# Latent attention with the rope query's two parts in one operand, a reordered beginning, FFN edges filled by needed transposes and a full-row bias matmul

## The chip, the cores and the metric

The kernel runs on one core of one Trainium2 chip. The metric is the device time of one execution in microseconds. A core has a matrix engine (TensorE, "PE" in the profile; its weight loads are the row "PEld"), a vector engine (VectorE, "DVE"), a scalar engine (ScalarE, "ACT"), GpSimd ("POOL") and SyncE ("SP"), whose queue issues the DMAs here. Each engine works through its own instructions in order; semaphores tie them together.

## What is computed

A decoder trunk of two layers on 256 tokens of width 1024, all in float32:

```
x <- LN(alpha*x + 0.5*SwiGLU_1(x))              # FFN 1, inner width 2816
x <- LN(alpha*x + Mixer(x))                     # layer 0: forgetting attention (FoX); layer 1: latent attention (MLA)
x <- LN(alpha*x + 0.5*SwiGLU_2(x))              # FFN 2
x <- LN(alpha*x + sigmoid(x Wg + bg) * (p Wp))  # per-layer embedding (PLE)
```

The latent attention has 16 heads. A head's score is a sum of two products: a query and a key of 128 columns each (no position), and a rotated query of 64 columns (rope) with a rotated key of 64 columns that all heads share:

```
c_q = rms_norm(x W_dq);  q = c_q W_uq                  # 16 heads x (128 + 64)
q_rope = rope(q[..., 128:]);  k_rope = rope(x W_kr)    # k_rope is shared by all heads
s = (q_nope . k_nope + q_rope . k_rope) / sqrt(192)    # causal softmax, then times V, then W_o
```

The keys without position and V come from a latent c_kv of 256 columns, formed once from the stream that leaves layer 0.

## The kernel before

**Arithmetic.** Each float32 operand is split into a high part (rounded to the matmul's input type, a copy on ACT) and a low part (the difference, a subtraction on DVE). `parts` (line 490) does this for activations. A product is then three matmuls into one PSUM bank: high x high, high x low, low x high (`mm3`, line 475; the instruction itself is line 483). Transposes are matmuls with an identity (line 487). The 256 tokens are two tiles t = 0, 1 of 128.

**Weights.** All weights stream from HBM once, in the order of their first use, which a dry run of the same program records. SP loads groups into three raw buffers; `Stream.split` (line 152) makes the high part on ACT (line 171) and the low part on DVE (line 172), into one of some ten slots. `pump` (line 240), called after each product, splits the next unit when it has arrived and ACT and DVE are, by a cost model in the source, not too far behind; `fill` (line 138) forces a number ahead; `ahead` (line 131) and `later` (line 147) do the two halves of a split at different places; `hold` forbids `pump`. PSUM has eight banks in three rings: `y` (4), `h` (2), `tr` (2).

**FFN** (`ffn`, line 572). The inner width is 11 chunks of 256. Chunks 0 and 1 are computed per token tile by `H`, with the tokens stationary, and transposed by `T` (line 630). Chunks 2 to 10 are computed by `HT` (line 642) with the weight stationary: four quarters u of 24 matmuls with 256 columns, into two banks of ring `h` (even chunks) or `tr` (odd chunks). `W` (line 668) multiplies a chunk with the output weight, 24 matmuls with 512 columns into the four `y` banks. The order is: H of 0 and 1, T(0), then three groups of three chunks (GROUPS, line 52), each followed by the W of the chunks done so far (0 to 4, then 5 to 7); the W of chunks 8 to 10 come last, for tile 0 and then tile 1, with the layer norms. T(1) stands inside chunk 2, behind its first quarter. Ahead of chunks 5 and 8, `HT` issues transposes of the identity that nobody reads: EDGE (line 53) has four each in FFN 1 and one each in FFN 2. In FFN 2 the PLE's input p is loaded at chunk 4, transposed at chunk 5 (`ple_transpose`, line 727) and projected at chunk 8 (`ple_project`, line 737; its copies to SBUF are line 750). In the FFN 1 of layer 1 the latent key side is transposed behind the first group (`kv_transpose`, line 1144).

**PLE** (`ple`, line 752). The gate's bias is added by two matmuls per block, with a row of ones as the stationary operand and the high and then the low part of the bias as one row (lines 756 to 763). Blocks are 512 columns, except four quarters of 256 for tile 1 of the last layer, whose eight bias matmuls stand together.

**Latent attention** (`mla`, line 1167). The beginning forms c_q (`dq`, `cq_transpose`), the rope queries (`q_rope`, `rope`; the sums of line 1237 are on GpSimd or DVE) and transposes them into `xT`, where high and low part are separate operands of 128 rows, two heads to an operand. `V` forms values, `gen(h)` (line 1242) query and key of head h. Then a loop over heads, written out by hand: gen(h+1), T(h-1) (transpose of the softmax's result P, line 1299), QK(h) (line 1260), softmax(h) (line 1276; its last step, line 1294, is on GpSimd), O(h-2) (product with the output weight, 12 matmuls), AV(h-1) (line 1316). QK has, for each of two query tiles (128 and 256 keys), three matmuls of query and key and three of rope query and rope key; the operand of the rope key is zero in the 64 rows of the pair's other head.

## Time and profile before

| | |
|---|---|
| runs shown | 1098.92, 1098.73, 1095.04 us; median 1098.73 |
| the profiled execution | 1100.22 us, its span 1098.2 us |
| mean granted TensorE clock | 0.997 |
| HBM read | 196.81 MB, 180 GB/s over the span |
| 16 DMA engines, share of the span on the weight queue | 55.6% |
| chain of work that ended last | PE 88%, DVE 5%, DMA 2%, ACT 2% |

In a row of a group, the names say output<-inputs, the shapes follow, then the count; behind the bar stand busy time in us, the mean length of one in ns, and the idle time of the engine just ahead of them with what ended it. The length of a matmul is longer than its distance to the next, because matmuls overlap in the array; the distance from start to start is what one costs. A row of the timeline has start, length in us, engine, line, operation, names and count. A row of the waits view has waiting engine, line and operation, the one waited for, us in total, times, and the longest.

### The profile page before, as it was taken

The page shows a single profiled execution, that of the slowest core. Times are in us where ns is not written, and L with a number is a line of the kernel's source. Part 1 is how long each engine was busy: PE and PEld are TensorE (multiplying, and loading weights), DVE is VectorE, ACT ScalarE, POOL GpSimd, SP SyncE. Part 2 cuts the span into 40 slices and gives each one's busy share as a digit, 9 for nine tenths or more (in the row PEclk, how much of TensorE's full clock was granted, in tenths as well). Part 3 has the DMA queues.
Part 4 walks back from the last instruction along what each step waited for, and adds up shares of the span by engine and source line. Part 5 has one row for each costly group of instructions (what it writes and reads, how often), then busy time and mean ns, then how long its engine had stood idle before and what let it go on. Part 6 is the DMA issues. An engine that isn't in the chain of part 4 may idle for free.

```text
span 1098.2 us, 17696 instructions
## 1 busy us (share of the span) xinstructions
PE 1080.7 (98%) x7186; PEld 978.4 (89%) x7186; DVE 713.3 (65%) x1010; ACT 542.2 (49%) x792; POOL 75.6 (7%) x126
## 2 busy tenths in 40 slices
PE   9999999999999999999999999999999999999997
PEld 6989999899879999997899899988999789898986
DVE  5765545788897545448976463487766885554576
ACT  5654443657645444434565353355655474444421
POOL 0000000223200000000220000011111000000000
PEclk9999999999999999999999999999999999999999
DMA  8886652454458766455577654444443578555502
GB/s 276 282 293 224 209 188 82 154 165 143 129 169 284 249 213 193 150 169 163 163 262 255 203 192 144 106 104 152 121 150 116 192 231 307 190 187 172 183 7 77
DMA packets 150676, 199.00 MB, mean 181 GB/s; under 512 B 11842, under 2 KB 128578, under 8 KB 150596
## 3 DMA queue, kind: packets, MB, share of 16 engines
q1 hardware_dynamic: 150596, 197.88, 55.6%
q8 instruction: 56, 0.92, 0.3%
q14 instruction: 24, 0.20, 0.1%
HBM read 196.81 MB, written 1.05 MB: 180 GB/s over the span
## 4 chain that ended last, share of the span: by engine, by line
PE 88%; DVE 5%; DMA 2%; ACT 2%; issue 1%; SPq 1%; POOL 1%; DVEq 0%; ACTq 0%; POOLq 0%
PE h L483 36%; PE y L483 31%; PE tr L483 19%; PE tr L487 2%; DMA raw<-in_ffn_w_in_dram 2%; DVE hl L172 2%; DVE x L560 1%; ACT hl L171 1%; DVE st L545 1%; DVE x L544 0%; SPq L319 0%; DMA x<-in_x_dram 0%; POOL rs L555 0%; PE tr L1009 0%; DMA raw<-in_mla_w_uq_dram 0%
## 5 line engine op out<-in xcount | busy, mean ns | idle before, releaser
L172 DVE TENSOR_TENSOR hl<-raw,hl 128x1024 fp32r<-128x1024 f32 (+3 forms) x287 | 334.5, 1188 | 167.9 <-ACT hl L171 167.0
L171 ACT ACTIVATE hl<-raw 128x1024 fp32r<-128x1024 f32 (+3 forms) x287 | 285.4, 1020 | 191.5 <-PE y L483 78.6
L483 PE MATMUL h<-xT,hl 128*128 128x256 f32 x2016 | 240.0, 278 | 1.5 <-DVE qk L493 0.9
L483 PEld LDWEIGHTS h<-xT,hl 128*128 128x128 f32 x2016 | 234.2, 188 | 3.5 <-DVE qk L493 1.1
L483 PE MATMUL y<-hl,g 128*128 128x512 f32 x816 | 189.6, 390 | 0.0
L483 PEld LDWEIGHTS y<-hl,g 128*128 128x128 f32 x816 | 152.2, 188 | 31.0
L483 PE MATMUL tr<-xT,hl 128*128 128x256 f32 x864 | 102.0, 277 | 0.0
L483 PEld LDWEIGHTS tr<-xT,hl 128*128 128x128 f32 x864 | 100.0, 188 | 0.1
L483 PE MATMUL h<-hl,xT 128*128 128x512 f32 (+1 forms) x396 | 94.8, 389 | 0.5 <-DVE hl L172 0.5
L483 PEld LDWEIGHTS h<-hl,xT 128*128 128x128 f32 x396 | 72.2, 188 | 17.2 <-DVE hl L172 2.0
L555 POOL TENSOR_TENSOR rs<-ve,mhalf 128x1 f32<-128x1 f32 x16 | 15.2, 951 | 829.7 <-DVE ve L554 829.7
L483 PE MATMUL y<-hl,xT 128*128 128x512 f32 (+2 forms) x312 | 61.3, 352 | 0.0
L483 PEld LDWEIGHTS y<-hl,xT 128*128 128x128 f32 x312 | 50.7, 188 | 8.0 <-issue 0.7
L492 ACT ACTIVATE xT<-tr 128x512 fp32r<-128x512 f32 x34 | 19.2, 597 | 59.6 <-PE tr L487 59.6
L493 DVE TENSOR_TENSOR g<-P,g 128x512 fp32r<-128x512 f32 x36 | 24.9, 692 | 34.5 <-ACT g L492 34.5
L492 ACT ACTIVATE g<-P 128x512 fp32r<-128x512 f32 x36 | 22.8, 634 | 40.0 <-DVE P L662 29.0
L172 DVE TENSOR_TENSOR otb<-raw,otb 128x1024 fp32r<-128x1024 f32 (+1 forms) x20 | 24.3, 1214 | 19.2 <-ACT otb L171 19.2
L483 PE MATMUL y<-hl,ota 128*128 128x512 f32 x144 | 36.4, 397 | 0.0
L172 DVE TENSOR_TENSOR qk<-raw,qk 128x1024 fp32r<-128x1024 f32 x21 | 25.7, 1224 | 11.4 <-ACT qk L171 11.2
L483 PE MATMUL tr<-xT,qk 128*128 128x256 f32 x264 | 31.9, 277 | 0.0
L483 PEld LDWEIGHTS tr<-xT,qk 128*128 128x128 f32 x264 | 30.9, 188 | 0.0
L483 PEld LDWEIGHTS y<-hl,ota 128*128 128x128 f32 x144 | 26.5, 191 | 5.0
(236 smaller groups left out, 1369.0 us busy)
## 6 DMA issues: line engine op xcount, KB each, us to landing
raw<-in_ffn_w_in_dram SPq DMA_DIRECT2D x172, 512.0 KB, 5.0
raw<-in_ffn_w_out_dram SPq DMA_DIRECT2D x44, 1024.0 KB, 5.1
raw<-in_fox_w_in_dram SPq DMA_DIRECT2D x12, 1024.0 KB, 5.2
raw<-in_ple_w_gate_dram SPq DMA_DIRECT2D x8, 1024.0 KB, 4.9
raw<-in_mla_w_o_dram SPq DMA_DIRECT2D x8, 1024.0 KB, 5.0
gb<-in_ln_g_dram SPq DMA_DIRECT2D x8, 512.0 KB, 6.5
gb<-in_ln_b_dram SPq DMA_DIRECT2D x8, 512.0 KB, 7.3
raw<-in_fox_w_o_dram SPq DMA_DIRECT2D x4, 1024.0 KB, 4.9
```

The source lines that it names most:

```text
L171: nc.scalar.activation(hi[:, c], src[:, c], AF.Copy)
L172: nc.vector.tensor_tensor(lo[:, c], src[:, c], hi[:, c].bitcast(F32), op=ALU.subtract)
L483: self.nc.tensor.matmul(out, lhsT, rhs, start=start, stop=stop)
L487: self.nc.tensor.transpose(out, in_, self.ident)
L492: self.nc.scalar.activation(hi, src, AF.Copy)
L493: self.nc.vector.tensor_tensor(lo, src, hi.bitcast(F32), op=ALU.subtract)
L545: nc.vector.bn_stats(st, xs)
L555: nc.gpsimd.tensor_tensor(rs, ve, self.mhalf, op=ALU.pow)
L560: nc.vector.scalar_tensor_tensor(xs, xs, rs if i else mv[:, 0:1], self.gb[:, i, hs[n]], op0=ALU.mult if i else ALU.subtract, op1=ALU.add i ...
```

## The change

1. *Rope scores.* The transposed rope queries are stored per head in one operand of 128 rows: the high part in the 64 rows of the head's place in its pair, the low part in the other 64. The rope key has three forms: its high part in both halves of the rows, and its low part in one half with zeros in the other, for even and for odd heads. QK then has two rope matmuls instead of three for each query tile. Since high and low part go to different rows, `zT_parts` makes them with two copies on ACT and two subtractions on DVE, on 64 partitions each, where one and one stood.
2. *Beginning of the latent attention.* The rope queries are formed in two halves of eight heads. Only the first half is transposed at the beginning; the second is rotated behind gen(2) and gen(3), and its eight transposes stand in T of heads 2 to 9, one in each. Low parts of V (and the scaling of c_q) are issued later than the high parts. QK and softmax of heads 0 and 1 stand ahead of V(2). Within softmax, both score segments are reduced before the first exponential. Splits at fixed places are set by I0 to I8, and in the loop `ahead` and `later` surround QK and softmax. The buffers change with it: the values' outputs for heads 0 to 9 rotate in four places.
3. *FFN edges.* The quarter u = 0 of a chunk goes bank by bank instead of alternating between its two banks. The identity transposes at the edges are gone, except four in FFN 1 of layer 0 ahead of chunk 8. T(1) stands ahead of chunk 5, W(1) behind the second group, and ahead of chunk 8 stand the four transposes of the latent key (FFN 1 of layer 1) or of the PLE's input (FFN 2). The PLE projection stands behind chunk 10, the load of p at chunk 6.
4. *Bias.* The stationary ones have 128 rows; the bias weight's slot is cleared by GpSimd, then the high part goes to row 0 and the low part to row 32. One matmul with 128 rows per block; in the last layer each quarter's bias stands ahead of that quarter.

The core of the diff:

```diff
 # Stream.split
+        elif key[0] == "pb":
+            nc.gpsimd.memset(w[:, 0, :].bitcast(F32), 0.0)
+            lo = w[32:33, 0, :n]
+            part(slice(None))
...
 # ffn
-EDGE = {(0, "ffn1"): 4, (0, "ffn2"): 1, (1, "ffn1"): 4, (1, "ffn2"): 1}
...
-            for _ in range(edge):
-                self.transpose(ps[0][:, 0:128], self.ident)
...
+                steps = [(kk, b) for kk in range(2) for b in range(4)]
+                if u == 0:
+                    steps.sort(key=lambda s: s[1] // 2)
...
+        late = [0, 2, 3, 4, 1] + list(range(5, n - STAG))
+        for i, group in enumerate(GROUPS):
+            if i == 1:
+                T(1, "h")
+            if i == 2:
+                if kv:
+                    self.kv_transpose()
+                elif ple:
+                    self.ple_transpose()
+                else:
+                    spare = self.bank("tr")
+                    for k in range(4):
+                        self.transpose(spare[:, 128 * k : 128 * k + 128], self.ident)
             for c in group:
...
-                HT(c, (lambda: T(1)) if c == 2 else None, EDGE[li, which] if c == group[0] > 2 else 0)
+                HT(c)
...
+            if i == 2 and ple:
+                self.ple_project(li)
...
 # ple
-                for i in range(2):
-                    self.mm(
-                        y[t, c0][:, 0 : c1 - c0], self.ones, w[0:1, i, c0:c1], i == 0, False
-                    )
+                self.mm(y[t, c0][:, 0 : c1 - c0], self.ones, w[:, 0, c0:c1], True, False)
...
 # mla
+        def zT_parts(t, h0, tr):
+            n = cols(tr) // 64
+            v = tr.rearrange("p (k c) -> p k c", c=128)
+            o = [zT[:, h0 + s : h0 + s + n - 1 : 2, 128 * t : 128 * t + 128] for s in range(2)]
+            r = [slice(0, 64), slice(64, 128)]
+            S.pair(128 * n)
+            for s in range(2):
+                nc.scalar.activation(o[s][r[s]], v[r[s]], AF.Copy)
+            for s in range(2):
+                nc.vector.tensor_tensor(o[s][r[1 - s]], v[r[s]], o[s][r[s]].bitcast(F32), op=ALU.subtract)
...
 # QK
-                self.mm3(
-                    b[:, c0:c1], lambda i: self.xT[:, q0 // 128, i, pair, :],
-                    lambda i: kr[:, i, 0:w], False, True,
-                )
+                for i in (0, 1 + h % 2):
+                    self.mm(b[:, c0:c1], zT[:, h, q0 : q0 + 128], kr[:, i, 0:w], False, i > 0)
...
 # the beginning, new order
+        dq(0)
+        V(0, (0, 1), late=lows)
+        self.XT(1, (0,))
+        dq_scale(0)
+        low()
+        V(1, (0,), "y", lows)
+        self.XT(1, (1,))
...
+        dq(1, 10, mid, 2)
+        z00 = q_rope(0, 0)
...
+        dq_scale(1)
+        rope(0, 0, z00)
+        V(1, (1,), "y", lows)
+        cq_transpose(1)
...
+        z01 = q_rope(0, 1)
...
+        z10 = q_rope(1, 0)
+        rope(1, 0, z10, True)
+        zT_half(0)
         gen(0)
...
+        gen(1)
...
+        zT_half(1)
...
+        z11 = q_rope(1, 1)
+        QK(0)
+        softmax(0)
...
+        QK(1)
+        softmax(1)
...
+        low()
+        V(2, (0,), "y", lows)
...
+        gen(2)
+        T(0)
+        rope(0, 1, z01)
+        gen(3)
...
+        AV(0)
+        rope(1, 1, z11)
+        low()
...
 # the loop
+            T(h - 1)
+            if h in EARLY:
+                S.ahead()
+            QK(h)
+            softmax(h)
+            S.later()
+            S.fill(AHEAD.get(h, AHEAD0))
```

More of the change, by code (lines that the diff above doesn't have):

```diff
@@ L431, in setup @@
         self.mhalf = one([128, 1], F32, "mhalf")
-        self.ones = one([1, 128], F32R, "ones")
+        self.ones = one([128, 128], F32R, "ones")
         self.xT = one([128, 2, 2, 8, 128], F32R, "xT")
@@ L703, in ffn @@
                     self.load_gb(li, lni)
-                HT(c, (lambda: T(1)) if c == 2 else None, EDGE[li, which] if c == group[0] > 2 else 0)
-            if kv and done == 0:
+                HT(c)
+            if i == 1 and kv:
                 self.flush()
-                self.kv_transpose()
-            while done < min(group[-1] + 1, n - STAG):
-                W(done, both)
-                done += 1
+                self.kv_transpose_rope()
+            if i == 2 and ple:
+                self.ple_project(li)
+            while late and (late[0] <= group[-1]) and not (i == 0 and late[0] == 1):
+                W(late.pop(0), both)
         for c in range(n - STAG, n):
@@ L793, in ple @@
         quarters = tuple((c, c + 256) for c in range(0, 1024, 256))
-        bias(1, full if not last else quarters)
         if not last:
+            bias(1, full)
             for k in range(8):
@@ L806, in ple @@
             for c0, c1 in quarters:
+                bias(1, ((c0, c1),))
                 for k in range(8):
@@ L1196, in V @@
                     )
-                o = self.tl([128, 2, 512], F32R, "g4", 5)
-                self.parts(o[:, 0, :], o[:, 1, :], ps)
-                v[t, g] = o
+                o = v[t, g] = self.tl([128, 2, 512], F32R, "g4", 5)
+                self.parts(o[:, 0, :], o[:, 1, :], ps, late)
         def cq_transpose(t):
-            b = self.bank("tr")
+            b = self.bank("h")
             for k in range(3):
@@ L1209, in cq_transpose, with q_rope @@
             )
-        def q_rope(t, at=None, what=None):
-            ps = [self.bank("y") for _ in range(2)]
+        def q_rope(t, n, at=None, what=None):
+            ps = self.bank("y")
             for k in range(3):
@@ L1286, in softmax @@
                 )
+            for q, (c0, c1) in enumerate(seg):
                 nc.scalar.activation(
@@ L1421, in run @@
         ple = lambda li: {
-            4: [keep("ota"), lambda: self.ple_load(li)],
-            5: [self.ple_transpose],
-            8: [lambda: self.ple_project(li)],
+            4: [keep("ota")],
+            6: [lambda: self.ple_load(li)],
         }
```

196 lines of the change are left out of this document (98 added, 98 removed).

## The prediction

> **What bounds the kernel now.** I read the page's totals first, then TensorE's waits, then busy time by stretch, then the timeline at the places the diff touches. From the page:
>
> ```profile
> span 1098.2 us, 17696 instructions
> PE 1080.7 (98%) x7186; PEld 978.4 (89%) x7186; DVE 713.3 (65%) x1010; ACT 542.2 (49%) x792; POOL 75.6 (7%) x126
> L483 PE MATMUL h<-xT,hl 128*128 128x256 f32 x2016 | 240.0, 278 | 1.5 <-DVE qk L493 0.9
> L483 PE MATMUL y<-hl,g 128*128 128x512 f32 x816 | 189.6, 390 | 0.0
> L483 PEld LDWEIGHTS y<-hl,g 128*128 128x128 f32 x816 | 152.2, 188 | 31.0
> ```
>
> TensorE (PE) is busy 98% of the span, in every stage. Busy time divided by count gives the price of one matmul in a stream: 240.0/2016 = 0.119 us at 256 columns, 189.6/816 = 0.232 us at 512. A matmul taken out of a full stream is therefore worth about its price; a reordering is worth only the idle time or slow pace that it removes. Of the idle time that the waits view names, one piece, TensorE's longest, lies where the diff reorders; the rows below it are five stretches with the busy time of PE, weight load, DVE, ACT and POOL, then the granted clock:
>
> ```profile
> PE h L483 <- ACT PT L492: 1.7, 1, 1.7
> ```
>
> ```profile
> 718.50:735.20 16.70, 16.40 (x93) 14.69 (x92) 15.36 (x24) 8.19 (x14) 1.54 (x2) 1.00 0.47 115
> 735.20:753.70 18.50, 17.62 (x98) 14.26 (x98) 17.55 (x32) 10.69 (x17) 3.15 (x3) 1.00 0.59 185
> 753.70:762.40 8.70, 7.00 (x58) 6.60 (x56) 4.88 (x15) 4.51 (x13) 0.96 (x3) 1.00 0.17 44
> 762.40:771.10 8.70, 8.48 (x45) 7.66 (x46) 5.97 (x13) 5.56 (x12) 1.53 (x4) 0.80 0.48 154
> 771.10:809.80 38.70, 38.70 (x273) 36.08 (x272) 27.88 (x58) 23.48 (x51) 4.58 (x10) 1.00 0.49 147
> ```
>
> The wait falls in the latent attention's beginning (718 to 771 us), in the stretch from 753.70, where PE is busy 7.00 of 8.70 us. VectorE (DVE) is 15.36/16.70 = 92% and 17.55/18.50 = 95% busy before it, so DVE paces that part; and after the wait the granted clock of the next 8.70 us is 0.80, which loses 0.20 x 8.70 = 1.7 us more. The loop over heads behind it (771 on) has TensorE always busy and DVE at 72%.
>
> **The change, part by part.** The sum is made against the profiled execution: 1100.2 us, 2.0 us more than its span of 1098.2, and 1.5 us over the median of the runs shown (1098.73).
>
> *Rope scores.* One head's score matmuls, from the timeline:
>
> ```profile
> 779.09 0.49 PE L487 MATMUL tr<-ident,P 128*128 128x128 f32 x3
> 779.34 0.53 PE L483 MATMUL tr<-qk 128*128 128x128 f32 x3
> 779.70 0.50 PE L483 MATMUL tr<-fs,xT 128*128 128x128 f32 x3
> 780.04 0.57 PE L483 MATMUL tr<-qk 128*128 128x256 f32 x3
> 780.44 0.51 PE L483 MATMUL tr<-fs,xT 128*128 128x256 f32 x3
> 780.79 1.08 PE L483 MATMUL y<-hl,ota 128*128 128x512 f32 x4
> ```
>
> From start to start, three rope matmuls of 128 columns take 0.34 us and three of 256 take 0.35. With the query's high and low parts in the rows of one operand, two of each three remain: 0.34/3 + 0.35/3 = 0.23 us a head, times 16 heads = **3.7 us**.
>
> *Bias matmuls.* Two one-row matmuls per block become one of 128 rows:
>
> ```profile
> 502.20 0.85 PE L483 MATMUL y<-hl,g 128*128 128x512 f32 x3
> 502.98 1.20 PE L483 MATMUL y<-fs,ones 1*128 1x512 f32 x4
> 504.11 1.65 PE L483 MATMUL y<-hl,xT 128*128 128x512 f32 x6
> 505.60 1.07 PE L483 MATMUL y<-qk,xT 128*128 128x512 f32 x4
> ```
>
> ```profile
> 1076.65 0.85 PE L483 MATMUL y<-hl,xT 128*128 128x512 f32 x3
> 1077.44 1.25 PE L483 MATMUL y<-hl,ones 1*128 1x256 f32 x8
> 1078.62 1.56 PE L483 MATMUL y<-hl,xT 128*128 128x256 f32 x11
> ```
>
> From 502.20 to 505.60 are 3 + 4 + 6 matmuls in 3.40 us. Without the switches to one row and back, and with two bias matmuls for four, 11 x 0.232 = 2.55: 0.85 us saved, at three places 2.55. The last layer's eight quarter blocks take 1.18 us and delay the neighbour before them by 0.1 (0.79 for three, against 0.70); four at 0.119 take 0.48, so 0.8. Together **3.35 us**. The Trainium skill (TensorE: Matmul & The Clock Gate, What overlaps and what doesn't) speaks against this edit: a weight load overlaps matmuls in flight only when their row groups differ. By that, ten full-row bias matmuls would each bare a load of 0.188 us, 1.9 us in all, and the sum below would be 1.9 smaller. The trace disagrees: 816 full-row matmuls follow each other at 0.232 us with an equal number of 0.188 us loads beside them.
>
> What the edit adds is a GpSimd memset of 128x1024 in front of the split of the bias weight, and ScalarE (ACT), with all its later splits queued behind, waits for it. No memset of that size is in the trace; the bias split itself is this:
>
> ```profile
> 469.99 1.21 DVE L172 TENSOR_TENSOR fs<-raw,fs 1x1024 fp32r<-1x1024 f32 x1 [1.59 <-ACT fs L171]
> ```
>
> It ends at 471.2 and its user starts at 502.98, so a memset between nothing and the length of that row (1.2, the same columns on DVE) is hidden by 31.8 us of FFN matmuls: I take 1.2 and cost it at nothing. Without that cover it would stand on the path in both layers, 2.4 us.
>
> *FFN, transposes.* At an edge of a group of weight-stationary chunks:
>
> ```profile
> 93.16 0.60 PE L487 MATMUL tr<-ident 128*128 128x128 f32 x4
> 93.51 11.15 PE L483 MATMUL tr<-xT,hl 128*128 128x256 f32 x96
> 104.50 0.73 PE L483 MATMUL h<-xT,hl 128*128 128x256 f32 x5
> ```
>
> Four dummies take 0.35 us plus about 0.1 by which the first chunk is slower: 96 in 10.99, where the next chunks need 96 x 0.1133 = 10.88. That is 0.11 us each. EDGE has 4+4+1+1 of them per layer, 20 in all; the change keeps four and lets transposes that are needed anyway stand at the other edges: 16 x 0.11 = **1.75 us**.
>
> *FFN, pace.* Behind that edge a 256-column matmul comes every 0.1133 us. The second FFN's last group is slower:
>
> ```profile
> 451.14 0.95 PE L483 MATMUL h<-xT,hl 128*128 128x256 f32 x6
> 452.29 8.04 PE L483 MATMUL h<-xT,hl 128*128 128x256 f32 x66 [0.20 <-ACT ota L750]
> ...
> 474.30 11.47 PE L483 MATMUL h<-xT,hl 128*128 128x256 f32 x96
> 485.61 1.55 PE L483 MATMUL y<-hl,g 128*128 128x512 f32 x6
> ```
>
> Its last chunk takes 11.31 us, 0.118 per matmul; it begins behind the PLE projection and one dummy, and waits for a bank. After the change it begins behind four transposes with both banks long free, as at 93.51, and should take 3 x 10.88 + 0.1 = 32.75 instead of 485.61 - 451.14 = 34.47: 1.7 us in each layer, 3.45. The projection now comes right behind the group and waits itself for the last chunk's SiLU to free its bank: nothing at best; at worst a full 0.8 us, two such waits as at 452.29 with the gap around it (0.34). I take 0.4 per layer. Net **2.65 us**.
>
> The first group has the same flaw in small:
>
> ```profile
> 335.57 3.12 PE L483 MATMUL h<-xT,hl 128*128 128x256 f32 x24
> 338.53 0.60 PE L487 MATMUL tr<-ident,P 128*128 128x128 f32 x4
> ```
>
> ```profile
> 896.40 0.94 PE L483 MATMUL h<-xT,hl 128*128 128x256 f32 x6
> 897.60 2.33 PE L483 MATMUL h<-xT,hl 128*128 128x256 f32 x18 [0.26 <-DVE P L627]
> ```
>
> Twenty-four matmuls take 2.96 us instead of 24 x 0.1133 + 0.1 = 2.82; in the last FFN the first six alone take 897.60 - 896.40 = 1.20 instead of 0.78, since the seventh needs a second bank that DVE still reads. The new order (bank by bank in the first quarter) needs it at the thirteenth, 0.7 us later. Three FFNs with 0.14, the last with 0.14 + 0.42: **1.0 us**. What is late next is the weight split, and that has run ahead.
>
> *Moved without a price.* The PLE load's two DMAs stand on SP's queue behind two more chunks' weights; their reader comes at least two chunks (21.8 us) later. W(1) goes behind the second group with its weight, whose place in the stream follows. The key's rope parts go past GpSimd and ACT one group later, and their first reader is 100 us off.
>
> *Beginning of latent attention.* DVE's queue is shortened: the low parts of V, the second half's rotation (two of four) and half of the query transposes go behind the first scores. Removable at most: the wait's 1.7 and the clock's 1.7, 3.4 us, if nothing new is late. At least nothing, since DVE's work is moved by 20 us rather than removed, and the first AV now stands behind two heads' softmax and five splits. A loss would need a wait as long as the one removed; that is the slower rival below. I take 2.5, above the middle, since the stretch that receives the work has DVE at 4.88/8.70 = 56%.
>
> *Loop.* T of heads 2 to 9 gets a fourth transpose, which costs what it saved at the beginning, and four small copies on 64 partitions. Halving the partitions saves no time:
>
> ```profile
> L1035 ACT ACTIVATE ota<-y 64x256 fp32r<-64x256 f32 x8 | 3.1, 382 | 0.0
> L492 ACT ACTIVATE ota<-h 128x256 fp32r<-128x256 f32 x8 | 3.0, 377 | 0.0
> ```
>
> At 128 columns these are below 0.38 each, so at most 0.8 us more on ACT and on DVE in a period of 6.9 us. DVE goes from 72% to 84%: hidden.
>
> Sum: 3.7 + 3.35 + 1.75 + 2.65 + 1.0 + 2.5 = 14.95. The profiled execution would take 1100.2 - 15 = 1085.2, a median 1098.7 - 15 = 1083.7; I forecast **1084**.
>
> **The rivals.** (1) *The beginning stays bound by DVE*, and a wait at the first AV replaces the one removed. For it: 92% and 95% above; against it: the room behind. The 2.5 us are gone and up to 1 us more: 1087.
>
> (2) *The FFN's pace does not hold.* Whether a stretch runs at 0.113 or 0.118 is decided at its start, and a short wait may turn the one into the other, as the 24 matmuls at 335.57 suggest. In the first groups no transposes stand in the middle any more to restore it. If the four first groups and the two last ones of the second FFN run at 0.118: 6 x 288 x 0.0045 = 7.8 us lost against the forecast: 1092. Against it: behind the four transposes at 93.16 all 96 of the next chunk keep 0.1133 but for 0.1 us at the start.
>
> (3) *It returns elsewhere* (the change does not do what it says): TensorE finishes earlier and waits for weight splits, so that the time hardly moves: 1096. Against it: the first two groups of matmuls quoted stand idle for 1.5 us and 0.0 in all.
>
> (4) *Slower.* The copies in T stand on ACT and DVE ahead of the softmax, whose result the next T needs:
>
> ```profile
> 776.48 1.26 POOL L1294 TENSOR_SCALAR P<-P,su 128x128 f32<-128x128 f32 x2 [6.54 <-DVE su L1292]
> ```
>
> It ends at 777.74, T starts at 779.09: 1.35 us of slack, less the 0.23 by which the period shrinks. If the copies delay the softmax by more than 1.1 us, each of eight heads waits. At the price of the wait at 762.4 with its clock (1.7 + 1.7 = 3.4), 8 x 3.4 = 27 us: 1111. Against it: the added work is at most 0.8 us on either engine, and both engines work side by side. The Trainium skill (TensorE: Matmul & The Clock Gate, What's actually happening) lets the clock fall only after about 3.4 us without work; by that, the eight waits cost 8 x 1.7 = 14 us: 1098. The trace disagrees: 0.80 after a wait of 1.7.
>
> **How the numbers follow.** Forecast 0.64, rival 1 0.16, rival 2 0.08, rival 3 0.08, rival 4 0.04. With all of the beginning's 3.4 us and no wait at the projection the forecast would be 1.7 us lower, 1082; the runs shown reach 3.7 us below their median (1095.04), so the low end is 1078. The high end takes in rivals 1 and 2: 1092. Half a per cent is 5.5 us, about what a measurement here can tell from no change: faster means below 1093.2, so 0.64 + 0.16 + 0.08 = 0.88; the same 0.08; slower 0.04.
>
> **What would show it.** TensorE's busy time should fall by about 12 us. A head's scores should take 0.98 us instead of 1.21, the bias rows read 128x512, the last chunk of the second FFN 10.9 us instead of 11.3, with no dummy left but four in the first FFN. The 1.7 us wait for PT should be gone and the clock 1.00 from 762 on. It is wrong if waits on PT, xT or P appear in heads 2 to 9, if chunks run at 0.118, or if the beginning holds a new wait over 1.5 us.

## The result, and the profile after

The changed kernel takes 1107.22 us (median of 4 runs, 1104.52 to 1111.19), the kernel before 1097.51 on the same chip (4 runs, 1095.04 to 1098.92). The ratio is 1.0101 with a 95% interval of 1.0083 to 1.0118: slower, on the other side of no change than the forecast of 1084. The profiled execution of after took 1104.52 us, its lowest; its page opens so:

```profile
span 1102.8 us, 17600 instructions
PE 1076.9 (98%) x7128; PEld 974.1 (88%) x7128; DVE 717.6 (65%) x1025; ACT 545.3 (49%) x807; POOL 99.4 (9%) x129
```

TensorE is busy for 3.8 us less, not 12 less as forecast, and the span is longer. What stands out is GpSimd: 99.4 us instead of 75.6 with three more instructions. The waits of TensorE name it too; it is the longest entry, and the wait for PT that the prediction started from is gone:

```profile
PE tr L496 <- POOL P L1336: 7.4, 9, 1.8
PE h L492 <- DVE hl L177: 1.5, 3, 1.0
PE y L492 <- DVE hl L177: 1.3, 1, 1.3
PE h L492 <- DVE qk L502: 1.2, 2, 0.9
```

**Where the time went, by stage.** From the trace's matmul starts, the first transpose of head 0 in the loop of latent attention comes at 750.41 us instead of 758.28: everything ahead of the loop together gained 7.9 us (the prediction's terms for that part sum to 7.5). From head 0's to head 15's transpose it takes 112.52 us instead of 97.81, where 94.1 was forecast. Behind that, 2.3 us were gained (forecast 3.8). The loop alone is worth more than the whole loss. Head 0 flatters the part ahead of it, though: by the first transpose of head 2 only 5.7 us of the 7.9 are left (766.46 instead of 772.18). The loop's steady part, from the transpose of head 2 to that of head 15, by busy time in a window (columns as in the prediction's rows of stretches); before:

```profile
772.18:856.09 83.91, 83.89 (x585) 77.62 (x584) 56.83 (x130) 50.43 (x118) 12.09 (x26) 1.00 0.41 126
```

and after:

```profile
766.46:862.93 96.47, 87.95 (x566) 77.37 (x566) 63.71 (x147) 57.17 (x136) 29.56 (x26) 0.98 0.45 141
```

Before, TensorE idled 0.02 of 83.91 us; after, 8.5 of 96.47, with 19 matmuls fewer, and the granted clock of 0.98 costs about another 2. GpSimd's 26 instructions take 29.56 us instead of 12.09. They are the scaling of P by the softmax's reciprocal, and the transposes T wait for it. Two heads, on GpSimd:

```profile
772.17 2.17 POOL L1336 TENSOR_SCALAR P<-P,su 128x128 f32<-128x128 f32 x2 [6.24 <-DVE su L1334]
779.97 3.47 POOL L1336 TENSOR_SCALAR P<-P,su 128x128 f32<-128x128 f32 x2 [5.62 <-DVE su L1334]
```

on VectorE:

```profile
771.84 0.17 DVE L1334 RECIPROCAL su<-su 128x2 f32<-128x2 f32 x1 [1.11 <-ACT P L1329]
771.92 1.20 DVE L192 TENSOR_TENSOR hl<-raw,hl 128x1024 fp32r<-128x1024 f32 x1
773.04 0.69 DVE L177 TENSOR_TENSOR hl<-raw,hl 128x512 fp32r<-128x512 f32 x1
...
779.63 0.17 DVE L1334 RECIPROCAL su<-su 128x2 f32<-128x2 f32 x1 [1.39 <-ACT P L1329]
779.76 0.96 DVE L192 TENSOR_TENSOR hl<-raw,hl 128x768 fp32r<-128x768 f32 x1
780.64 2.44 DVE L177 TENSOR_TENSOR hl<-raw,hl 128x1024 fp32r<-128x1024 f32 x2
```

and on TensorE:

```profile
774.70 0.53 PE L492 MATMUL tr<-qk 128*128 128x128 f32 x3
775.07 0.39 PE L492 MATMUL tr<-fs,xT 128*128 128x128 f32 x2
775.29 0.57 PE L492 MATMUL tr<-qk 128*128 128x256 f32 x3
775.70 0.40 PE L492 MATMUL tr<-fs,xT 128*128 128x256 f32 x2
775.93 2.94 PE L492 MATMUL y<-hl,otb 128*128 128x512 f32 x12
...
782.07 0.33 PE L496 MATMUL tr<-ident,P 128*128 128x128 f32 x1 [0.20 <-POOL P L1336]
783.49 0.44 PE L496 MATMUL tr<-ident,P 128*128 128x128 f32 x2 [1.09 <-POOL P L1336]
```

The reader sees three things. The scores are shorter as forecast: from the first score matmul to O 1.23 us instead of 1.45. The pair of scalings, 1.26 us in the prediction's row, takes 2.17 and 3.47. In the single records behind these rows the first scaling of each pair ends at 773.89 and at 782.02, each time 0.16 us behind the end of VectorE's second split of weights (773.73 and 781.86). And those splits now start right behind the reciprocal, since `ahead` and `later` put ScalarE's half of a split ahead of the scores; before, VectorE first waited there for ScalarE, in the same two heads:

```profile
776.68 3.00 DVE L172 TENSOR_TENSOR hl<-raw,hl 128x512 fp32r<-128x512 f32 x3 [0.29 <-ACT hl L171]
784.01 2.74 DVE L172 TENSOR_TENSOR hl<-raw,hl 128x1024 fp32r<-128x1024 f32 x3 [0.72 <-ACT hl L171]
```

### The profile page after: what moved, and what is told of

It reads as the page before. It is cut to its first block, busy times and chain, and to the rows that moved or that the text cites. A ratio compares the mean times of both kernels' runs of the same rounds, so it can differ in the third digit from the quotient of the medians.

```text
span 1102.8 us, 17600 instructions
## 1 busy us (share of the span) xinstructions
PE 1076.9 (98%) x7128; PEld 974.1 (88%) x7128; DVE 717.6 (65%) x1025; ACT 545.3 (49%) x807; POOL 99.4 (9%) x129
## 4 chain that ended last, share of the span: by engine, by line
PE 84%; DVE 8%; ACT 3%; POOL 2%; issue 2%; DMA 1%; SPq 0%; DVEq 0%; ACTq 0%; POOLq 0%
PE h L492 35%; PE y L492 30%; PE tr L492 17%; DVE hl L177 2%; POOL P L1336 2%; PE tr L496 2%; ACT P L1329 1%; DMA raw<-in_ffn_w_in_dram 1%; DVE x L573 1%; DVE tr L1324 1%; DVE PT L502 1%; DVE st L558 1%; ACT hl L176 1%; DVE x L557 1%; DVE qk L502 0%
## 5 line engine op out<-in xcount | busy, mean ns | idle before, releaser
L177 DVE TENSOR_TENSOR hl<-raw,hl 128x1024 fp32r<-128x1024 f32 (+3 forms) x275 | 321.5, 1188 | 155.9 <-ACT hl L176 155.1
L176 ACT ACTIVATE hl<-raw 128x1024 fp32r<-128x1024 f32 (+3 forms) x275 | 275.3, 1022 | 190.0 <-PE y L492 89.7
L492 PE MATMUL h<-xT,hl 128*128 128x256 f32 x2064 | 244.3, 278 | 0.9 <-DVE qk L502 0.9
L492 PEld LDWEIGHTS h<-xT,hl 128*128 128x128 f32 x2064 | 239.7, 188 | 2.1 <-DVE qk L502 1.1
L492 PE MATMUL y<-hl,g 128*128 128x512 f32 x780 | 181.0, 390 | 0.0
L492 PEld LDWEIGHTS y<-hl,g 128*128 128x128 f32 x780 | 145.7, 188 | 29.8
L492 PE MATMUL y<-hl,otb 128*128 128x512 f32 x168 | 44.2, 406 | 1.5 <-DVE hl L177 1.3
L1336 POOL TENSOR_SCALAR P<-P,su 128x128 f32<-128x128 f32 (+1 forms) x32 | 35.1, 1110 | 82.1 <-DVE su L1334 82.1
L492 PEld LDWEIGHTS y<-hl,otb 128*128 128x128 f32 x168 | 30.9, 192 | 8.7 <-DVE hl L177 1.6
L501 ACT ACTIVATE g<-P 128x512 fp32r<-128x512 f32 x36 | 22.8, 632 | 30.8 <-DVE P L673 30.8
L177 DVE TENSOR_TENSOR qk<-raw,qk 128x1024 fp32r<-128x1024 f32 x21 | 25.8, 1229 | 12.7 <-ACT qk L176 12.7
L177 DVE TENSOR_TENSOR otb<-raw,otb 128x1024 fp32r<-128x1024 f32 (+1 forms) x20 | 24.1, 1203 | 12.6 <-ACT otb L176 12.6
L672 ACT ACTIVATE P<-h 128x512 f32<-128x512 f32 x20 | 12.0, 599 | 37.8 <-PE h L492 37.8
```

The lines of the kernel that those rows point to most:

```text
L176: nc.scalar.activation(hi[:, c], src[:, c], AF.Copy)
L177: nc.vector.tensor_tensor(lo[:, c], src[:, c], hi[:, c].bitcast(F32), op=ALU.subtract)
L492: self.nc.tensor.matmul(out, lhsT, rhs, start=start, stop=stop)
L501: self.nc.scalar.activation(hi, src, AF.Copy)
L672: nc.scalar.activation(gt, ps[0], AF.Silu)
L1336: nc.gpsimd.tensor_scalar(P[:, c0:c1], P[:, c0:c1], su[:, q : q + 1], 1.0, op0=ALU.mult, op1=ALU.mult)
```

## The experiments

The experiments are numbered; a number below stands for the kernel of that experiment. Two theories stood first. A: the order of splits and softmax makes GpSimd late. B (rival 4): the copies in T stand ahead of the softmax on VectorE and ScalarE. The stretch from head 2's to head 15's transpose is the measure.

**1. The order undone.** Diff: `EARLY = range(2, 15)` becomes `EARLY = ()`.

> The changed kernel with EARLY empty: no early high half of a split ahead of QK and no late low half behind the softmax in the head loop; all other parts stay. Theory A (the low half of the early split stands on VectorE right behind the reciprocal, and GpSimd's scaling of P, which starts 0.25 us later, gets nothing done while VectorE subtracts SBUF from SBUF): the first scaling of a head falls from a mean of 1.48 us to under 0.6, the 7.4 us in which TensorE waits for GpSimd vanish, and the time falls to 1084 to 1090. Rival B (the copies added to T fill ACT and VectorE ahead of the softmax): the waits stay above 5 us and the time stays above 1100.

Measured: 1103.48 us, ratio to before 1.0058 [1.0043, 1.0073].

```profile
770.40:863.59 93.19, 85.49 (x567) 75.63 (x566) 64.25 (x148) 53.94 (x135) 16.05 (x26) 1.00 0.42 129
```

GpSimd is nearly back to its old busy time, but 3.3 us of 12.6 are all that return. Theory A alone, which gave 1084 to 1090, is not enough.

**2. The scaling on ScalarE**, as an activation with a scale in place of GpSimd's operation.

> The changed kernel with the two scalings of P on ScalarE instead of GpSimd; EARLY and the copies in T stay. Theory A: ACT is not held up by VectorE, so the waits for P's scaling fall under 1 us in all and the time falls to 1085 to 1094, somewhat less of a gain than without EARLY if ACT's queue delays other copies. Rival B: ACT gets still more work, the waits for P stay or grow, 1105 or more.

Measured: 1106.23, 1.0075 [1.0058, 1.0092]; the stretch 93.45 us. TensorE's wait for GpSimd is gone, and waits for VectorE and ScalarE stand in its place. Taking GpSimd out doesn't mend the loop; it gives the same 3 us as undoing the order.

**3. No copies in T.** Diff: the second half of the rope queries is transposed and copied ahead of the loop by `zT_parts`, and not in T.

> The changed kernel with the second half of the rope queries transposed and copied ahead of the loop, so that T has three transposes and no copies; EARLY stays. Theory A: GpSimd's scaling stays at a mean above 1.2 us and TensorE still waits over 4 us for it, time 1100 to 1110. Rival B: the waits vanish, 1085 to 1092.

Measured: 1104.68, 1.0069 [1.0051, 1.0087].

```profile
778.46:865.59 87.13, 83.27 (x559) 74.76 (x557) 59.07 (x133) 52.46 (x120) 29.76 (x27) 1.00 0.51 159
```

The stretch falls by 9.3 us: the copies, and the transposes that moved with them, were the larger part. The whole gains little, since heads 0 to 2 take 22.0 us instead of 16.1: the copies ahead of the loop wait for GpSimd's rope additions (5.2 us of TensorE's waits), and the granted clock is 0.50 for 10.24 us, from 764.04 on, instead of 3.41.

**4. The order alone, in the kernel before.** Diff: `S.ahead()` ahead of QK and `S.later()` behind softmax, for heads 2 to 14.

> The kernel before with one thing added: the early high half ahead of QK and the late low half behind the softmax, for heads 2 to 14. Theory A: the scaling of P is stretched from 0.37 and 0.48 us to a mean of over 1 us, the next T waits in most heads, and the time rises by 8 to 20 us. Rival B (the early split does no harm by itself): within 3 us of the kernel before.

Measured: 1103.63, 1.0056 [1.0041, 1.0071].

```profile
770.13:861.50 91.37, 85.82 (x584) 77.65 (x583) 57.44 (x130) 52.55 (x119) 30.24 (x26) 1.00 0.43 136
```

With no other edit the order costs 7.5 us in the stretch, and GpSimd goes from 12.09 to 30.24 us. The only waits of TensorE there are 5.1 us for GpSimd's P, in five heads. So A is shown for its part, though the whole rose by 6.7 us and not by the 8 or more that A gave.

**5. Both undone.** Diff: 1 and 3 together.

> The changed kernel with the rope queries' second half transposed and copied ahead of the loop, and with the softmax in its old place in VectorE's order (nothing moved ahead of the splits). It undoes both suspects at once. From the first transpose of head 2 to that of head 15: before 83.91 us, after 96.47; with the copies out alone 87.13, with the order undone alone 93.19. Theory A (two separate costs, the copies' share of VectorE's queue and GpSimd's scaling of P that stands still while VectorE subtracts from SBUF to SBUF): 81 to 84 us, so that the shorter scores come through. Rival (the loop is slow for a third reason, such as the new score operand or its reads): 87 us or more. The eight copies ahead of the loop wait for GpSimd's rope additions, so that the first two heads stay about 8 us longer than before and the whole is about 1096 to 1102 by A.

Measured: 1100.59, 1.0021 [1.0010, 1.0032].

```profile
773.19:857.70 84.51, 82.41 (x559) 74.91 (x558) 58.90 (x132) 49.72 (x119) 13.03 (x26) 1.00 0.46 142
```

The two by two is closed: 96.47 with both, 93.19 and 87.13 with one, 84.51 with neither. The copies cost 8.7 to 9.3 us, the order 2.6 to 3.3 beside the other edits. (Seven transposes left the stretch with the copies, some 0.8 us of this at the prediction's 0.11 each.) With neither the stretch is about as long as before, so the shorter scores still bring nothing over the whole of it. Up to head 9 the period is 6.72 us instead of 6.91; heads 9 to 13 then take 25.8 instead of 23.6, waiting for splits of weights. What keeps the whole from falling below before is heads 0 to 2, 22.8 us instead of 13.9: TensorE waits there for GpSimd's rope additions (4.8 us) and for the copies (2.2), and the granted clock is 0.50 from 755.97 to 769.63, which loses 6.8 us where before loses 1.7.

**6. The low copies behind the softmax.** Diff: as 1, and the two subtractions of `zT_parts` in T are issued behind softmax(h).

> The changed kernel with the softmax in its old place in VectorE's order, and with the low parts of the query copies in T (two subtractions on VectorE) behind the softmax of the next head instead of ahead of it; no work is left out. Theory of VectorE's queue (its busy time and its waits for ScalarE inside the chain of a head add up to the period of 6.9 us): from the first transpose of head 2 to that of head 15 83 to 87 us instead of 96.47, and GpSimd's scaling of P near 0.4 and 0.8 us; whole 1088 to 1096. Rival (the copies cost by their mere amount on VectorE, wherever they stand, or by ScalarE's half): 90 us or more, whole 1098 to 1103.

Measured: 1099.26, 1.0006 [0.9996, 1.0015]; the stretch 88.04 us. The same work, later in VectorE's queue, gives 5.2 of the copies' 8.7 us back: more of their cost is their place than their amount. (The stretch lies between the two forecasts, 83 to 87 and 90 or more; the whole lies where the rival put it.) Why a queue that is some 70% busy has no room is argued from heads 2 to 9, before, by a window (behind the length stand PE, weight load, then VectorE) and by the waits of VectorE:

```profile
772.18:820.53 48.35, 48.35 (x338) 45.00 (x337) 33.49 (x74) 29.76 (x67) 6.67 (x14) 1.00 0.50 153
```

```profile
DVE su L1292 <- ACT P L1287: 4.9, 7, 0.7
DVE hl L172 <- ACT hl L171: 4.2, 7, 0.7
DVE tr L1283 <- ACT P L1287: 4.1, 7, 0.6
DVE qk L493 <- ACT qk L492: 1.6, 3, 0.7
```

and after, the same two:

```profile
766.46:823.17 56.71, 50.92 (x330) 44.68 (x330) 39.56 (x89) 35.49 (x83) 18.46 (x14) 0.99 0.45 135
```

```profile
DVE su L1334 <- ACT P L1329: 8.1, 7, 1.4
DVE xT L1275 <- ACT xT L1273: 4.4, 7, 0.6
DVE PT L502 <- ACT PT L501: 2.5, 4, 0.8
DVE qk L502 <- ACT qk L501: 1.9, 3, 1.3
```

Before, VectorE is busy 33.5 us of the 48.35 and waits 14.8 for ScalarE. After, it is 39.6 busy and 16.9 waiting, of 56.71. That the two fill the stretch proves nothing, since an idle engine always waits for something; what counts is for whom. Of the 14.8 us before, 13.2 lie between steps of the softmax and of the splits, which VectorE and ScalarE take in turn, and only the 1.6 for qk lead back to TensorE (ScalarE waits for it there). One head's low copies on VectorE add 0.59 of work and 0.62 of waiting for ScalarE's high copies:

```profile
769.22 0.59 DVE L1275 TENSOR_TENSOR xT<-tr,xT 64x128 fp32r<-64x128 f32 x2 [0.62 <-ACT xT L1273]
```

That is 1.21 us a head, and experiment 1, with the copies, has a mean period of 7.79 us from head 2 to head 9 against 6.73 in experiment 5 without them: 1.06 more. Nearly all of the added time shows, so there was next to no room for it.

**7 and 8. The FFN.** Seven: before with only the FFN and bias edits. Eight: kernel 6 with four identity transposes ahead of every group of chunks that has none.

> Only the edits of the FFN's transposes, its order of banks, and the bias matmuls of 128 rows; the latent attention is that of the kernel before. By the prediction's own terms: 3.35 + 1.75 + 2.65 + 1.0 = 8.75 us less than before, 1088. Rival (the pace of a group of three chunks is decided at its edge, and without dummy transposes some groups run at 118 ns a matmul, 1.26 us a group): four to eight slow groups of twelve give 5 to 10 us back, 1092 to 1097, with a wide spread of runs.

> The kernel of the late copies (old softmax order, low parts of the copies behind the softmax), with four dummy transposes of the identity right in front of each group of FFN chunks that has none. They cost 11 x 0.35 = 3.9 us. Theory of the pace (a group behind four dummies always runs at 113 ns): all twelve groups take 32.7 us, and against the kernel of the late copies the time changes by 3.9 less 1.26 for each slow group that it has: with four to eight slow ones 1 to 6 us shorter. Rival (the pace is not decided there): the dummies only cost, 4 us longer, and slow groups stay.

A group is 288 matmuls with 256 columns. At 113.3 ns from start to start it takes 32.74 us, at 117.8 ns ("at 118") 34.00, so a slow group costs 1.26 us; a program has 12 groups. Measured: seven 1095.5, 0.9966 [0.9954, 0.9978], with 3 groups of 12 at 118 ns; eight 1104.18, 1.0049 [1.0031, 1.0066], with 4 at 118 ns in spite of the transposes. So the transposes cost their time and didn't make every group fast: the theory of eight falls. They weren't without effect: the four slow groups of six (the first of layer 0's second FFN, the last of layer 1's first, the first two of its second) are fast in eight, and four others are slow, the first two of either FFN 1, in one execution of each.

Seven is a test of four terms of the sum, 8.75 us together, and 3.1 came. In its profiled execution three slow groups cost 3.8 us where the forecast had none, and the granted clock is 0.50 for 6.83 us, from 761.35 on, instead of 3.41, which is 1.7 more.

**9 to 12. One part alone, and a better kernel.** Nine: before with the score operand alone, all copies ahead of the loop. Ten: before with the bias matmuls, the PLE's transposes ahead of the second FFN's last group and its projection behind it. Eleven: both. Twelve: eleven with `AHEAD[11] = 4`.

> The kernel before with the score operand alone: high and low parts of the rope queries in the rows of one operand, two rope matmuls for three, all sixteen heads' copies made ahead of the loop, where before made them (each set of four transposes now with two copies of 64 partitions on ScalarE and two on VectorE, in place of one each of 128). By the prediction's price of 0.23 us a head: 3.7 us less in the loop, from the first transpose of head 2 to that of head 15 81 us instead of 83.9; the four additional copies of about 0.64 us stand on VectorE, which paces the beginning, so up to 2.6 us back: whole 1095 to 1097.5 against 1098.6. Rival (TensorE then waits for the splits of weights, as heads 9 to 13 do in the kernel without copies and without the new order, 25.8 us instead of 23.6): the loop 83 us or more, whole 1098 to 1100.

> The kernel before with the 128-row bias matmuls, and with the embedding's transposes at the edge of the second FFN's last group and its projection behind that group; all other dummy transposes stay, and the latent attention is that of before. By the prediction's terms: 3.35 for the bias and 2.2 to 2.9 for the last group of each second FFN (34.5 to 33.0 us, less the wait at the projection), 5.5 to 6 us less: 1092.5 to 1093.5. Rival (the bias rows are worth less than worked out, or the projection waits longer): 1094 to 1097.

> The kernel with the bias and embedding edits and the score operand together, all copies ahead of the loop. If the parts add: the gain of either kernel alone, summed; 1089 to 1092. Rival (what the shorter scores give comes back as waits for the splits of weights): the same as the kernel with the bias and embedding edits alone, within 1 us.

> The kernel with the bias and embedding edits and the score operand, with one number changed: behind the scores of head 11 the splits may run four weights ahead instead of three, so that the split of the 768-column query weight comes one head earlier. Theory (the shorter scores are lost at heads 11 to 13 because that split now comes later than its matmuls): from the first transpose of head 11 to that of head 13 10.9 us instead of 14.3, the clock's drop behind the wait gone, whole 1094 us, about the same as the kernel with the bias and embedding edits alone, because the copies ahead of the loop cost 2.6 us. Rival (the weight itself arrives late, or ScalarE has no room for the split there): the wait moves to another head and the whole stays at 1097.

Measured: nine 1102.24, 1.0025 [1.0016, 1.0034]; ten 1094.77, 0.9955 [0.9942, 0.9967]; eleven 1097.17, 0.9983 [0.9973, 0.9993]; twelve 1097.21, 1.0000 [0.9990, 1.0010]. In nine (its profiled execution, 1099.26, is its fastest) the period of a head is 6.69 us instead of 6.91, 0.22 less, which is the prediction's price. But head 0 comes 2.6 us later behind the last FFN chunk (57.34 instead of 54.78), and heads 11 to 13 take 14.3 instead of 11.2, waiting for a split, so that the stretch from head 2 to head 15 takes 85.35 us, more than before's 83.91. In twelve that wait is gone (12.07; 10.9 was expected), and the whole is no shorter. Ten beats both kernels, and eleven is 2.4 us slower than ten: the operand with all its copies ahead of the loop costs more than it saves.

**13. GpSimd by itself.** A block ahead of the kernel before: three scalings of 128x256 alone, beside VectorE with both sources in SBUF, beside VectorE with one in PSUM, beside ScalarE.

> The kernel before with a block of work added at its start, whose results nothing reads: three scalings by GpSimd of 128x256 in SBUF, as the loop has them, once with nothing beside, once beside VectorE subtractions with both sources in SBUF, once beside VectorE subtractions with one source in PSUM, once beside ScalarE copies in SBUF; the four cases twice. Only the durations of the block's own instructions are read. Theory A (GpSimd gets nothing done while VectorE reads both sources from SBUF): about 0.45 us for a scaling alone, beside a PSUM source and beside ScalarE, and beside the four SBUF subtractions (4.6 us in all) the first or second scaling lasts as long as they do, 4 us or more. Rival (GpSimd is only late because VectorE's reciprocal releases it late, or because of ScalarE): all four cases alike within 0.1 us.

On GpSimd:

```profile
4.86 1.39 POOL L473 TENSOR_SCALAR P<-P,su 128x256 f32<-128x256 f32 x3
6.53 4.22 POOL L473 TENSOR_SCALAR P<-P,su 128x256 f32<-128x256 f32 x3 [0.28 <-DVE su L470]
11.97 1.39 POOL L473 TENSOR_SCALAR P<-P,su 128x256 f32<-128x256 f32 x3 [1.23 <-DVE su L470]
17.77 1.39 POOL L473 TENSOR_SCALAR P<-P,su 128x256 f32<-128x256 f32 x3 [4.41 <-DVE su L470]
```

on VectorE:

```profile
6.35 5.46 DVE L478 TENSOR_TENSOR qk<-ota,otb 128x1024 fp32r<-128x1024 f32 x4
...
11.85 5.76 DVE L480 TENSOR_TENSOR qk<-y,otb 128x512 fp32r<-128x512 f32 x8
```

Alone, beside a PSUM source and beside ScalarE three scalings take 1.39 us; beside subtractions from SBUF 4.22. Single records show one scaling per subtraction (1.38, 1.44, 1.44 us, each ending 0.35 us behind the end of a subtraction), where theory A had expected one scaling to last through all four. Theory A's mechanism is shown. The Trainium skill (SBUF — State Buffer, SBUF: two separate sides) states that a VectorE operation with two SBUF inputs and a GpSimd operation that reads SBUF lock each other out of a shared port pair: the one that starts first has it for its whole instruction. The trace agrees, and the prediction did not weigh it. In the loop it is worse than turn by turn. The block's subtractions start 0.03 us behind each other's end; in the loop the next starts some 0.08 us before the last has ended, and there the first scaling waits for two of them (772.17 to 773.89 and 779.97 to 782.02 above).

**14 and 15. Places of tiles.** In run 13 the FFN groups came slow with the FFN code of before (the expectation counts 11 of 12; by their means all 12 lie between 117 and 118.5 ns, with single chunks from 113 to 119). Fourteen: its tiles without its instructions. Fifteen: such a block in tiles that are there anyway.

> The kernel before, with the tiles of the added block made at its start and no instruction of it (they have the names of tiles that the kernel uses later, so only the places of tiles in SBUF and their turns can shift). In the run with the whole block 11 of 12 groups of FFN chunks came at 118 ns a matmul though their code is that of before. Theory of places (where the operands lie decides the pace): most groups at 118 ns here too, the whole about 12 us or more over before. Rival (the later start decides it, or chance in each execution): at most 2 slow groups, the whole as before.

> The kernel before, with a block of about the same length at its start (GpSimd scalings alone and beside VectorE's subtractions) that works in tiles which the kernel has there anyway, so that no place shifts. Theory of places: at most 2 groups of FFN chunks at 118 ns. Rival (the start's delay decides the pace): most groups at 118 ns. The scalings themselves: 0.48 us alone, 1.4 us beside the subtractions, as in the run with the whole block.

Measured: fourteen 1116.61, 1.0166 [1.0136, 1.0195], all 12 groups slow, with means from 117 to 118.5 ns; fifteen 1132.25, 1.0308 [1.0278, 1.0338], the block's own 30 us and more, 1 group (its scalings 1.38 and 4.21 for three). The page of fourteen, and its row for the FFN matmuls, 8.0 us more than before:

```profile
span 1114.3 us, 17696 instructions
PE 1097.7 (99%) x7186; PEld 992.5 (89%) x7186; DVE 713.4 (64%) x1010; ACT 541.7 (49%) x792; POOL 75.4 (7%) x126
L493 PE MATMUL h<-xT,hl 128*128 128x256 f32 x2016 | 248.0, 283 | 0.9 <-DVE qk L503 0.5 <-ACT ota L760 0.4
```

The same instructions take 18 us longer because tiles are asked for earlier, which moves them in SBUF (and can shift the turns of those that rotate); a later start does nothing.

**16 and 17. The places of before.** The change asks for g4 earlier, which moves hl9, ota and otb. Sixteen: the changed kernel with the tiles asked for in before's order. Seventeen: the same for kernel seven.

> The changed kernel, instruction for instruction, with its tiles in SBUF laid out in the order of the kernel before (the change asks for the five g4 tiles ahead of the last weight slot and of ota and otb, which moves these three). Theory of places (the operands' places decide how often a group of FFN chunks comes at 118 ns a matmul): at most 2 slow groups of 12 instead of 3 to 7, and a median 3 to 5 us lower than that of the changed kernel: 1102 to 1104.5 against 1107.2, ratio about 1.006. Rival (the edges of the groups decide, as the prediction had it): 3 or more slow groups, 1105 to 1108, ratio 1.008 to 1.011.

> The kernel with only the FFN and bias edits (latent attention of before), with its tiles in the order of the kernel before. It had 3 slow groups and 0.9966. Theory of places: at most 2 slow groups, 3 us lower: 1091 to 1093, ratio 0.993 to 0.995, the best of all. Rival (the edges decide): as before, 1095.5, 0.9966.

Measured: sixteen 1105.51, 1.0092 [1.0074, 1.0109], 5 groups at 118 ns; seventeen 1095.1 (1090.87 to 1096.92 in 12 runs), 0.9991 [0.9978, 1.0003], 4 groups. The rival holds: before's order of tiles doesn't restore the pace. Both matter. Over the profiles, without those of 8, 13 and 14, with before's edges (in ten to twelve all but the PLE's) and order of tiles 6 of 84 groups run at 118 ns, with the change's edges 37 of 108, whichever the order of tiles. They are not spread evenly over those nine profiles: the last group of layer 1's FFN 1, behind the latent key's transposes, is slow in all nine and the first group of its FFN 2 in eight, while the last groups of layer 0's two FFNs are slow in none. Why is not shown.

## Why the prediction was wrong

**The step that failed** is "*Loop.* ... at most 0.8 us more on ACT and on DVE in a period of 6.9 us. DVE goes from 72% to 84%: hidden." The 0.8 bound on the work was right (0.59). Hidden it was not. The added work brings 0.62 us of waiting for ScalarE's copies with it, 1.21 in all, and it stands ahead of the softmax in a queue where VectorE and ScalarE already take turns: the share in which VectorE did not work was mostly waits between these turns, and not room. Kernels 3 and 5 price the copies at about 9 us with their transposes, and kernel 6 shows that 5.2 of it hang on the place of the two subtractions. Busy share was read where the waits view of VectorE had to be read with it.

**How far that goes.** Profile against profile 19.3 us are missing (1104.52 instead of 1085.2): 18.4 in the loop, 1.5 behind it, and 0.4 the other way ahead of it. In the loop copies and order together are 12.0 (96.47 less the 84.51 of kernel 5); 3.6 are scores that got shorter without the stretch doing so (84.51 instead of 83.91 less 13 x 0.23); about 2.9 lie in heads 0 to 2.

**What was left out**: the order of `ahead`, softmax and `later` has no term in the sum. It costs 2.6 to 3.3 us here and 7.5 in the kernel before, with GpSimd locked out by VectorE's splits. Rival 4 named the place (T waits for P) and the engines, and its 1111 is near the 1107 measured, but by a price that was too high: it had 3.4 us for each of eight waits, and the stretch of 13 heads lost 12.6 us, about 1 us each. That the two lie so near is luck in part.

**What held.** *Rope scores*: 0.22 us a head against 0.23, where the loop is not delayed. (The lengths given as signs, 0.98 and 1.21 us, don't follow from the prediction's rows, which give 1.45 before and 1.22 after; 1.23 was measured.) *Bias*: the rows

```profile
498.47 1.64 PE L492 MATMUL y<-hl,g 128*128 128x512 f32 x6
499.94 0.62 PE L492 MATMUL y<-fs,ones 128*128 128x512 f32 x2
500.40 1.54 PE L492 MATMUL y<-hl,xT 128*128 128x512 f32 x6
501.77 1.53 PE L492 MATMUL y<-qk,xT 128*128 128x512 f32 x6
```

show two bias matmuls in 0.46 us, from their start to the next row's, and three, two and six matmuls at about 2.6 us, near the 2.55 worked out (3.40 for three, four and six before). The clearing of the slot took 0.96 us, hidden. *FFN*: the last group of layer 0's second FFN took 32.97 us instead of 34.47; 32.75 was worked out. Layer 1's ran at 118 ns as before.

**What held only in part** is the beginning, and the FFN's pace. *Beginning*: from the last FFN chunk to head 0 it takes 3.9 us less (50.88 instead of 54.78). By the prediction's own prices 0.46 of this are two heads' scores and some 0.9 the eight transposes that now stand in T, which leaves the 2.5 forecast. But from head 0 to head 2, before and after,

```profile
758.28:772.18 13.90, 11.99 (x74) 10.80 (x73) 9.80 (x21) 7.45 (x18) 1.80 (x5) 0.88 0.40 124
750.41:766.46 16.05, 12.33 (x72) 10.36 (x71) 13.42 (x25) 8.73 (x20) 7.33 (x6) 0.92 0.20 66
```

TensorE idles 3.7 us instead of 1.9, now waiting for splits of weights (1.3, 1.1 and 1.0 us), and the clock still falls. 2.2 us go back, so almost nothing is gained by head 2. This is rival 1 in kind, other waits in place of the one removed, though they stand at weights and not at the first AV.

*FFN*. Rival 2's premise was right (a group keeps one pace from its start, but for the kernels with moved tiles, and the change's edges lose the fast one more often), its likelihood too low: the profile of after has three groups at 118 ns, 3.8 us, and kernels with its edges 2 to 7. This also fits why after's runs lie up to 6.7 us apart; other executions than the profiled one were not seen inside. What decides a single group stays open: neither transposes ahead (8), nor the start (15), nor the order of tiles alone (16, 17) settles it, though tiles moved further do harm it (14). Rival 3 came too: in kernels 5, 9 and 11 shorter scores return as waits for splits.

## What to carry to other kernels

Before adding work to an engine in a loop, look at what its idle time is: waits for an engine that in turn waits for this one are no room, and the work that is added brings such waits of its own. Then undo the work in a run and compare the period. Look, too, which engine's operation follows a split on VectorE: GpSimd work that reads SBUF should not start beside a run of VectorE operations with two SBUF sources. An edit that moves tiles or edges needs its FFN pace measured, group by group and over several executions, since slow groups are worth several us in all.

## What the runs showed of the hardware

- GpSimd and VectorE lock each other out when VectorE has two SBUF sources. Where each subtraction starts behind the end of the one before, they alternate, one whole instruction each: a 0.48 us scaling takes 1.38 to 1.44, and a subtraction goes from 1.22 to 1.38 us (single records of 13 and 15). Where the next subtraction starts before the last has ended, a scaling waits for both: 1.72 and 2.05 us instead of 0.37 for 128x128 in the loop of after. One source in PSUM, or ScalarE beside it, leaves the scaling at 0.48.
- The place of tiles in SBUF (or their turns) alone changes the pace of matmuls with 256 columns from 113 ns to a mean of 117 to 118.5 over a group; the kernel before went from 1098.34 to 1116.61 us (14).
- A short idle halves the granted clock for 3.41 us and costs 1.7 us. In after, in three windows of that length:

```profile
757.76:761.17 3.41, 3.25 (x16) 2.32 (x15) 2.78 (x9) 0.50 (x3) 1.30 (x1) 1.00 0.00 0
761.17:764.58 3.41, 1.46 (x7) 1.25 (x8) 2.90 (x5) 2.88 (x6) 2.56 (x2) 0.88 0.10 28
764.58:768.00 3.42, 3.42 (x21) 3.42 (x21) 2.09 (x3) 1.08 (x2) 1.35 (x1) 0.62 0.92 215
```

0.12 x 3.41 + 0.38 x 3.42 = 1.7 us are lost, with 1.95 us of idle in the second window; from 763.78 to 767.19 the granted clock is 0.50. In kernel 5 it stays at 0.50 for four such lengths (755.97 to 769.63), in which TensorE is busy 8.5 us of 13.7. The Trainium skill (TensorE: Matmul & The Clock Gate, What's actually happening) gives a window of 3.413 us that runs freely; the length agrees.
